# Low parts of feed-forward weight blocks: ScalarE and an adding transfer in VectorE's place, and 12 more blocks in seven products

## The chip, the cores and the metric

One core of one Trainium2 chip runs the whole program. The metric is the device time of one execution in microseconds; the time of a kernel is the median of its runs. The core has TensorE (PE: matmuls, and PEld, the weight loads beside them), VectorE (DVE), ScalarE (ACT), GpSimd (POOL) and SyncE (SP), which run side by side, each in the order of its own queue, and wait for one another by semaphores. Transfers are issued from a queue (before: SP's, and two from ACT's) and carried by 16 DMA engines.

## The reference

Two layers over x of 512 tokens by 1024 features, float32. Each has three sub-layers with a norm, a shift and scale made from a conditioning vector c, and a gated residual: a SwiGLU feed-forward, a mixer (convolutions in the first layer, pooling and block attention in the second), and a feed-forward again. Then a last norm. What the change touches is the feed-forward:

```python
def swiglu(h, w_gate, w_up, w_down):
    return (jax.nn.silu(h @ w_gate) * (h @ w_up)) @ w_down
...
mod = (cond @ ada_w[i] + ada_b[i]).reshape(bn, N_SUBLAYERS, 3, D_MODEL)
h = modulate(rms_norm(x, ffn_norm[i, 0]), mod[:, 0, 0], mod[:, 0, 1])
x = x + 0.5 * mod[:, 0, 2][:, None, :] * swiglu(h, ffn_w_gate[i, 0], ffn_w_up[i, 0], ffn_w_down[i, 0])
```

There are four feed-forwards, with 2816 inner columns (22 blocks of 128), in this order: layer 0 before and after the convolutions, layer 1 before and after the attention. The text calls them the first to the fourth.

## The kernel before

Activations lie transposed, features on partitions, 512 tokens along the row. A product in float32 is made of three matmuls in fp32r: each operand is split into a high part (rounded) and a low part (the rest), and high x high, high x low and low x high are summed in PSUM (`mac`, lines 299 to 301). `split` makes the parts of a weight block: ScalarE casts the raw block to `whi` (line 284), then VectorE subtracts to give `wlo` (line 286).

A feed-forward runs in three sections of 8, 6 and 8 blocks (`SECTIONS`): in each, gate and up products make the section's columns (`th`, `tl`), then eight down products (d0 to d7) add to the residual `x` (line 988). An *item* is one such product: 8 (or 6) k-steps of three matmuls over 512 tokens. Some blocks of a section are instead run as a *pair* (`pair_run`): gate and up of one block taken together as a two-by-two block product in seven products in place of eight (a11, s2, s3, a12, s1, a22, s4; `seventh`, line 784, matmuls over 256 tokens). That needs sums of weight blocks (lines 762, 766, 770), splits of them (741, 744, 749, 753), and steps on the results: `u2` (VectorE, line 840, the text's u, then two ScalarE copies to `yy`, 842 and 843, after which s1 may write its bank), `cc` (847), the multiply (859). It also needs four operand *forms* of the activations per feed-forward (`forms`, lines 723 to 735). `pair_items` says how many blocks of each section are pairs: (0, 2, 8), (2, 6, 8), (2, 4, 8) and (2, 6, 8) for the four feed-forwards, 56 in all. The rest of a section's gate and up blocks come first, as items.

The order of the work is written out in a plan, and `run` walks it. Before each plan step it splits the weights of items up to three ahead (`AHEAD`), as far as the four weight buffers (`W_BUFS`) allow: a product's buffers are those of the product four before. Raw weights come in a ring of four tiles of 1 MB (`RAW_BUFS`), filled by SP in the order of first use; a tile is reloaded when its last reader is done. The modulation vectors (c times `ada_w`) of later sub-layers are made in the background: `ada_steps` gives four accumulating steps (lines 482, 484), a `fold` (497, 498) and a small matmul per 1024 columns, and `beside` and `slack` put them on VectorE between items, by a credit per item (`free`, in microseconds of the author's estimate) less each step's cost. None is put in while pairs run (`hold`). `lead_in` starts a section's first pair, in the last four items before it.

`boundary` carries one sub-layer into the next: the last down products in halves, the statistics (`stats`, with POOL's power of -1/2, line 554), and the new h (`apply`).

Of the kernel before, what the change touches and what calls it, by code (L numbers as in the profile page):

```python
# [8 lines left out]
F32 = mybir.dt.float32  # L9
F32R = mybir.dt.float32r  # L10
AF = mybir.ActivationFunctionType
ALU = mybir.AluOpType
# [30 lines left out]
class Item:  # L43


    def __init__(self, raw, cut, shape, post=None, rhs=None, korder=None, store=None):
        self.raw, self.cut, self.shape = raw, cut, shape
        self.post, self.rhs = post, rhs
        self.korder, self.store = korder, store
        self.hi = self.lo = self.ps = None  # L50
        self.left = 0
        self.pool_low = self.late = self.hold = False


class Pair:
# [13 lines left out]
class Trunk:  # L69
# [200 lines left out]
    def split(self, it):  # L270
        nk, m = it.shape
        src = it.cut(it.raw.tile)
        if it.store is None:
            parts = [[p.tile([P, 1024], F32R, name=n, tag=n)[:, 0:nk * m].rearrange(
                "p (a b) -> p a b", a=nk) for p, n in ((self.wp, "whi"), (self.wp, "wlo"))]]
            step = nk
        else:
            parts = [[t.rearrange("p (a b) -> p a b", b=m) for t in pair] for pair in it.store]
            step = S // m
        it.hi, it.lo = [], []  # L280
        for i, (hi, lo) in enumerate(parts):
            w = src[:, i * step:(i + 1) * step, :]
            n = w.shape[1]
            self.nc.scalar.copy(hi[:, 0:n, :], w)  # L284
            eng = self.nc.gpsimd if it.pool_low else self.nc.vector
            low = lambda eng=eng, lo=lo, hi=hi, w=w, n=n: eng.tensor_tensor(  # L286
                lo[:, 0:n, :], w, hi[:, 0:n, :].bitcast(F32), op=ALU.subtract)
            if it.hold:
                self.held.append(low)
            else:  # L290
                low()
            it.hi += [hi[:, a, :] for a in range(n)]
            it.lo += [lo[:, a, :] for a in range(n)]
# [235 lines left out]
    def square(self, k, sl):  # L529

        nc = self.nc
        if k == 0:
            nc.scalar.activation(self.acc[:, sl], self.x[k][:, sl], AF.Square)
            return
        sq = self.np_.tile([P, S], F32, name="sq", tag="sq")
        nc.scalar.activation(sq[:, sl], self.x[k][:, sl], AF.Square)
        if self.ending and k == 7 and sl.start > 0:
            self.sq7 = sq
            return
        self.defer(lambda: nc.vector.tensor_tensor(  # L540
            self.acc[:, sl], self.acc[:, sl], sq[:, sl], op=ALU.add))

    def stats(self, half):
        nc = self.nc
        ps = self.bank()
        for j in range(2):
            c = 2 * half + j
            terms = [self.acc] if half == 0 or not self.ending else [self.acc, self.sq7]
            for t in terms:
                nc.tensor.matmul(ps[:, j:j + 1], lhsT=t[:, c * P:(c + 1) * P], rhs=self.ones[:, 0:1],  # L550
                                 start=t is terms[0], stop=t is terms[-1])
# [265 lines left out]
    def pair_run(self, pairs, down):  # L817
# [15 lines left out]
                self.plan.append(("use", slot))  # L833

        def keep1(p):
            p.p1 = self.fp.tile([P, 256], F32, name="p1c", tag="p1c", bufs=1)
            nc.scalar.copy(p.p1, p.ab[:, 0:256])

        def u2(p):
# [95 lines left out]
    def beside(self, items, todo, bg, free):  # L935
# [9 lines left out]
            self.slack(bg, free - cost)  # L945
        self.room = len(bg)

    def swiglu_pairs(self, secs, pairs, bg, skip, fn=None, due=0):


        self.form, self.credit, self.room = {}, 0.0, len(bg)
        end = len(bg) - due
        forms = [(lambda kk=kk: self.call(lambda: self.forms(kk)), 4.6) for kk in range(4)]
        lead = [list(zip(self.lead_in(ps[0]), (2.5, 1.4, 1.9, 1.2))) if ps else [] for ps in pairs]
        for n, ((gu, down), ps) in enumerate(zip(secs, pairs)):
            nf, last = SECTIONS[n], n == len(secs) - 1
            gu = gu[skip if n == 0 else 0:2 * (nf - len(ps))]
            todo = lead[n] if gu else []
            if n == 0 and ps:
                todo = forms + [(None, 0)] * (len(gu) - 8) + todo  # L960
            self.beside(gu, todo, bg, 3.7)
            if n == 0:
                assert len(bg) <= end
                self.plan.append(("sync",))
            if ps:
                self.plan.append(("hold", True))
                self.pair_run(ps, down)
                self.plan.append(("hold", False))
                self.slack(bg, 3.0)
            if fn is not None and last:  # L970
                self.call(lambda: self.table(fn))
            todo = []
            if not last and len(pairs[n + 1]) == SECTIONS[n + 1]:
                todo = lead[n + 1]
            if n == 0 and not ps:
                todo = forms + todo
            self.beside(down[2 if ps else 0:6 if last else 8], todo, bg,
                        2.9 if last else 3.5 if nf == 8 else 2.3)
        self.plan.append(("sync",))
        while bg:  # L980
            self.call(*bg.pop(0)[:2])
            self.call(self.flush)
# [163 lines left out]
    def group_norm(self, r):  # L1146
        nc = self.nc
        _, j, y, stage, x = r
        if stage == 0:
# [1 line left out]
            nc.tensor.matmul(ps, lhsT=self.blk, rhs=y, start=True, stop=True)  # L1151
            nc.vector.tensor_tensor(y, y, ps, op=ALU.subtract)
            self.free(ps)
            r[4] = sq = self.np_.tile([P, S], F32, name="sq", tag="sq")
            nc.scalar.activation(sq, y, AF.Square)
        elif stage == 1:
            ps = self.bank()
# [8 lines left out]
            r[4] = wide = self.np_.tile([P, S], F32, name="sq", tag="sq")  # L1166
# [115 lines left out]
    def pool_post(self, g):  # L1282
        nc = self.nc

        def go(ps, sl):
# [7 lines left out]
            w = 2 << g  # L1293

            def mean():
                o = self.np_.tile([P, S], F32, name="sq", tag="sq")
                nc.vector.scalar_tensor_tensor(o, cur[:, 16:], 1.0 / w, u[:, 16:],
                                               op0=ALU.mult, op1=ALU.subtract)
                nc.vector.tensor_tensor(o[:, 0:w], cur[:, 16:16 + w], self.rcnt[:, 0:w], op=ALU.mult)
                nc.vector.tensor_tensor(o[:, 0:w], o[:, 0:w], u[:, 16:16 + w], op=ALU.subtract)  # L1300
                self.defer(lambda: mix(o), 2)

            def mix(o):
                po = self.bank()
                nc.tensor.matmul(po, lhsT=self.pw[:, g, :], rhs=o, start=True, stop=True)
                b, sc = self.at["pool_b"] + g, self.at["pool_scale"] + g
                m = self.np_.tile([P, S], F32, name="sq", tag="sq")
# [163 lines left out]
    def start_spread(self):  # L1471
        nc = self.nc
        ps = self.bank()
        for c in range(4):
            nc.tensor.transpose(ps[:, c * P:(c + 1) * P],
                                self.rs[0][:, c:c + 1].to_broadcast([P, P]), self.ident)
        self.rb0 = self.np_.tile([P, S], F32, name="sq", tag="sq")
        nc.scalar.copy(self.rb0, ps)
        self.free(ps)

# [43 lines left out]
    def build(self):  # L1524
# [63 lines left out]

        bg = steps(0, (0, 2), (1, 1), (1, 0), (1, 2), (2, 1), (2, 0))
        bg.insert(6, (self.rest, None, 0.6))  # L1590
        self.swiglu_pairs(f[0, 0], self.pair_items(0, 0, (0, 2, 8)), bg, 7, AF.Sigmoid, 9)

        self.boundary_tail(f[0, 0], 1, z[:4])
        self.taps1, self.taps2, self.ready = [], [], []
# [26 lines left out]
        self.boundary(zo[6:], 2, g0[0][0][:4])  # L1621

        bg = steps(1, (0, 1), (0, 0), (0, 2))
        self.swiglu_pairs(g0, self.pair_items(0, 2, (2, 6, 8)), bg, 3)
        self.boundary(g0[-1][1][6:], 3, f[1, 0][0][0][:4], False)
        bg = steps(1, (1, 1), (1, 0), (1, 2), (2, 1))
        self.swiglu_pairs(f[1, 0], self.pair_items(1, 0, (2, 4, 8)), bg, 3, AF.Exp)

        self.boundary_tail(f[1, 0], 4, kq[:4])
        self.call(self.pm_consts)  # L1630
# [23 lines left out]
        self.mm(po[4])  # L1654
        self.mm(po[5])
        self.boundary(po[6:], 5, f[1, 2][0][0][:4])
        self.swiglu_pairs(f[1, 2], self.pair_items(1, 2, (2, 6, 8)), [], 3)
        tail = f[1, 2][-1][1][6:]
        self.call(lambda: setattr(self, "ending", True))
        self.call(lambda: self.scaled(range(5), FULL))  # L1660
# [99 lines left out]
```

## Time and profile before

| what | value |
|---|---|
| median of 3 runs | 1872.02 us (1871.92 to 1874.3) |
| the profiled execution | 1867.62 us, its span 1865.6 us |
| granted TensorE clock, mean | 0.989 of full speed |
| TensorE, VectorE, ScalarE, POOL busy | 97%, 77%, 43%, 7% |
| DMA | 247.52 MB, mean 133 GB/s, queue of SP 42.5% of 16 engines' span |

All times of the trace are in microseconds from the start of the span, those of single instructions partly in ns. The page gives busy shares of each engine, then the span in 40 slices of 46.6 us, then the chain of work that ended last, then groups of instructions by line. An engine's idle time in front of an instruction is put down to what released it.

### The profile page before, as it was taken

The numbers are of one execution on the slowest core, as the hardware profiler recorded it, in microseconds if no ns is written. First come the engines' busy times: TensorE is split into PE (matmuls) and PEld (weight loads), VectorE is DVE, ScalarE is ACT, GpSimd is POOL, SyncE is SP. The second block draws the span as 40 slices with busy tenths as digits, with TensorE's granted clock in tenths as the row PEclk, the third lists the DMA queues.
The fourth block names the chain that finished last, engine by engine and source line by source line (L and its number), as shares of the span: only waits on it lengthen the run. The fifth ranks groups of instructions, "written<-read, shape, count | busy, mean of one in ns | idle before, by whom it ended". The sixth has DMA issues, their size and how long they took to land.

```text
span 1865.6 us, 26636 instructions
## 1 busy us (share of the span) xinstructions
PE 1803.4 (97%) x10730; PEld 1566.0 (84%) x10730; DVE 1438.5 (77%) x2100; ACT 802.3 (43%) x1388; POOL 133.9 (7%) x107
## 2 busy tenths in 40 slices
PE   5999999999979999999999999999999999999998
PEld 4778889988758888989888889998876688898997
DVE  6689779788988868779678787886898577485874
ACT  4322335445544433535344234463545444253543
POOL 2100000005550000000000000000002000000000
PEclk7999999999989999999999999999999999999999
DMA  9585563433232346453423573543362132424321
GB/s 258 169 290 198 161 204 101 136 113 113 68 136 91 113 158 181 133 139 113 149 77 114 191 226 119 156 124 111 125 208 80 45 91 68 113 80 125 91 91 46
DMA packets 263234, 247.52 MB, mean 133 GB/s; under 512 B 5212, under 2 KB 243656, under 8 KB 263112
## 3 DMA queue, kind: packets, MB, share of 16 engines
q1 hardware_dynamic: 262980, 245.78, 42.5%
q8 instruction: 84, 1.38, 0.3%
q14 instruction: 38, 0.31, 0.0%
q10 hardware_dynamic: 132, 0.05, 0.0%
HBM read 243.72 MB, written 2.10 MB: 132 GB/s over the span
## 4 chain that ended last, share of the span: by engine, by line
PE 82%; DVE 12%; ACT 3%; issue 2%; POOL 1%; DMA 0%; SPq 0%; DVEq 0%; ACTq 0%; POOLq 0%
PE bank L784 27%; PE bank L299 17%; PE bank L301 17%; PE bank L300 17%; DVE hl L577 1%; DVE wlo L286 1%; DVE bank L1111 1%; PE bank L1378 1%; DVE wlo L753 1%; DVE t L572 1%; DVE adaacc L484 1%; ACT whi L284 1%; DVE s L762 1%; DVE acc L1501 1%; DVE yb L1043 0%
## 5 line engine op out<-in xcount | busy, mean ns | idle before, releaser
L299 PE MATMUL bank<-th,whi 128*128 128x512 f32 (+1 forms) x896 | 336.3, 375 | 5.2 <-ACT whi L284 4.5
L301 PE MATMUL bank<-th,wlo 128*128 128x512 f32 (+1 forms) x896 | 332.8, 371 | 5.4 <-POOL wlo L286 5.4
L300 PE MATMUL bank<-tl,whi 128*128 128x512 f32 (+1 forms) x896 | 332.8, 371 | 1.1 <-DVE tl L680 0.9
L299 PE MATMUL bank<-hh,whi 128*128 128x512 f32 (+1 forms) x864 | 322.3, 373 | 5.3 <-ACT hh L575 3.2
L300 PE MATMUL bank<-hl,whi 128*128 128x512 f32 (+1 forms) x864 | 316.8, 367 | 8.0 <-DVE hl L577 8.0
L301 PE MATMUL bank<-hh,wlo 128*128 128x512 f32 (+1 forms) x864 | 315.9, 366 | 2.5 <-DVE wlo L286 2.5
L284 ACT CAST whi<-raw 128x1024 fp32r<-128x1024 f32 (+1 forms) x205 | 203.9, 1010 | 136.3 <-PE bank L300 83.2
L286 DVE TENSOR_TENSOR wlo<-raw,whi 128x1024 fp32r<-128x1024 f32 (+1 forms) x195 | 235.0, 1220 | 26.5 <-ACT whi L284 25.7
L301 PEld LDWEIGHTS bank<-th,wlo 128*128 128x128 f32 x896 | 169.0, 189 | 38.5 <-POOL wlo L286 6.6
L299 PEld LDWEIGHTS bank<-th,whi 128*128 128x128 f32 x896 | 169.1, 189 | 38.0 <-ACT whi L284 5.6
L300 PEld LDWEIGHTS bank<-tl,whi 128*128 128x128 f32 x896 | 169.2, 189 | 32.2 <-DVE tl L680 1.3
L300 PEld LDWEIGHTS bank<-hl,whi 128*128 128x128 f32 x864 | 164.0, 190 | 37.9 <-DVE hl L577 9.5
L299 PEld LDWEIGHTS bank<-hh,whi 128*128 128x128 f32 x864 | 163.5, 189 | 37.5 <-ACT hh L575 3.3
L988 DVE SCALAR_TENSOR_TENSOR x<-bank,modG,x 128x512 f32<-128x512 f32 (+1 forms) x124 | 85.7, 698 | 141.1 <-PE bank L301 140.1
L301 PEld LDWEIGHTS bank<-hh,wlo 128*128 128x128 f32 x864 | 163.6, 189 | 32.2 <-DVE wlo L286 3.7
L784 PE MATMUL bank<-f,whi 128*128 128x256 f32 x896 | 163.7, 280 | 11.2 <-ACT yy L843 11.2
L784 PE MATMUL bank<-f,qhi 128*128 128x256 f32 x896 | 165.3, 282 | 0.0
L741 ACT CAST qhi<-raw 128x512 fp32r<-128x512 f32 x168 | 99.4, 618 | 118.4 <-issue 84.4
L784 PEld LDWEIGHTS bank<-f,whi 128*128 128x128 f32 x896 | 136.8, 188 | 13.4 <-ACT yy L843 13.4
L484 DVE SCALAR_TENSOR_TENSOR adaacc<-raw,cond,adaacc 128x1024 f32<-128x1024 f32 x112 | 143.7, 1283 | 2.7
L784 PEld LDWEIGHTS bank<-f,qhi 128*128 128x128 f32 x896 | 138.8, 190 | 0.0
L784 PE MATMUL bank<-f,qlo 128*128 128x256 f32 x448 | 126.4, 282 | 0.0
(245 smaller groups left out, 3317.8 us busy)
## 6 DMA issues: line engine op xcount, KB each, us to landing
raw<-in_ada_w_dram SPq DMA_DIRECT2D x64, 1024.0 KB, 5.3
raw<-in_ffn_w_down_dram SPq DMA_DIRECT2D x32, 1024.0 KB, 5.2
raw<-in_ffn_w_gate_dram SPq DMA_DIRECT2D x58, 512.0 KB, 4.0
raw<-in_ffn_w_up_dram SPq DMA_DIRECT2D x58, 512.0 KB, 5.3
raw<-in_ffn_w_gate_dram SPq DMA_DIRECT2D x15, 1024.0 KB, 5.4
raw<-in_ffn_w_up_dram SPq DMA_DIRECT2D x15, 1024.0 KB, 5.4
raw<-in_ffn_w_down_dram SPq DMA_DIRECT2D x16, 768.0 KB, 4.5
raw<-in_conv_w_in_dram SPq DMA_DIRECT2D x10, 1024.0 KB, 5.0
```

The costliest lines, as they stand in the source:

```text
L284: self.nc.scalar.copy(hi[:, 0:n, :], w)
L286: low = lambda eng=eng, lo=lo, hi=hi, w=w, n=n: eng.tensor_tensor(lo[:, 0:n, :], w, hi[:, 0:n, :].bitcast(F32), op=ALU.subtract)
L299: nc.tensor.matmul(ps, lhsT=it.hi[k], rhs=xh[:, sl], start=start, stop=False)
L300: nc.tensor.matmul(ps, lhsT=it.hi[k], rhs=xl[:, sl], start=False, stop=False)
L301: nc.tensor.matmul(ps, lhsT=it.lo[k], rhs=xh[:, sl], start=False, stop=stop)
L484: nc.vector.scalar_tensor_tensor(acc, r.tile[:, j, :], self.cond[:, k:k + 1], acc, op0=ALU.mult, op1=ALU.add)
L572: nc.vector.scalar_tensor_tensor(t, self.x[k][:, sl], self.modA[:, i, k:k + 1], rb, op0=ALU.mult, op1=ALU.mult)
L577: self.pend = lambda: nc.vector.scalar_tensor_tensor(self.hl[k][:, sl], t, b, self.hh[k][:, sl].bitcast(F32), op0=ALU.add, op1=ALU.subtract)
L741: self.nc.scalar.copy(hi, src)
L753: p.lows[names] = lambda: self.nc.vector.tensor_tensor(lo, src, hi.bitcast(F32), op=ALU.subtract)
L784: mm = lambda w, x, start=False: nc.tensor.matmul(ps, lhsT=w, rhs=x, start=start, stop=False, skip_group_check=True)
L988: nc.vector.scalar_tensor_tensor(self.x[d][:, sl], ps[:, sl], self.modG[:, i, d:d + 1], self.x[d][:, sl], op0=ALU.mult, op1=ALU.add)
```

## The change

For 116 items (`by_dma`: in each feed-forward the gate and up items of the first section from the fifth on, but in the first one from the ninth, and all down products) the low part is made otherwise: ScalarE writes -w, rounded, into `wlo`, and a transfer issued from POOL adds the raw block to it in place, SBUF to SBUF, which leaves w less its high part. The counts of pairs become (0, 6, 8), (4, 6, 8), (4, 6, 8) and (4, 6, 8), 68 in all. The credits per item rise by about one. `join` packs forms and lead-in where fewer items are left than they had. Some tiles move between pools, and the area for the descriptors of such transfers grows from 1024 to 4096 bytes a partition.

```diff
@@ split
-            if it.hold:
+            if it.by_dma:
+                self.nc.scalar.activation(lo[:, 0:n, :], w, AF.Copy, scale=-1.0)
+                self.nc.gpsimd.dma_start(lo[:, 0:n, :], w, accum_op=ALU.add)
+            elif it.hold:
                 self.held.append(low)
@@ square: a full-width square goes to a tile with tag "yy", a half to one of 256 columns
@@ pair_run
-            p.p1 = self.fp.tile([P, 256], F32, name="p1c", tag="p1c", bufs=1)
+            p.p1 = self.np_.tile([P, 256], F32, name="t256", tag="t", bufs=3)
@@ new
+    def join(self, forms, lead, n):
+
+        gap = n - len(forms) - len(lead)
+        if gap >= 0:
+            return forms + [(None, 0)] * gap + lead
+        out = [(None, 0)] * (n - 4) + lead
+        for e, (fn, cost) in enumerate(forms):
+            k = e * (n - 3) // len(forms)
+            f0, c0 = out[k]
+            if k < n - 4:
+                out[k] = (lambda a=f0, b=fn: (a and a(), b()), c0 + cost)
+            else:
+                last = forms[e:]
+                out[k] = (lambda b=f0: ([f() for f, _ in last], b()), c0 + cost * len(last))
+                break
+        return out
@@ swiglu_pairs
+        for it in secs[0][0][max(skip + 1, 4):] + sum((gu * (n > 0) + down for n, (gu, down) in enumerate(secs)), []):
+            it.by_dma = True
...
-                todo = forms + [(None, 0)] * (len(gu) - 8) + todo
-            self.beside(gu, todo, bg, 3.7)
+                todo = self.join(forms, todo, len(gu))
+            self.beside(gu, todo, bg, 4.7)
...
-                        2.9 if last else 3.5 if nf == 8 else 2.3)
+                        4.0 if last else 4.6 if nf == 8 else 3.2)
@@ build
-        self.swiglu_pairs(f[0, 0], self.pair_items(0, 0, (0, 2, 8)), bg, 7, AF.Sigmoid, 9)
+        self.swiglu_pairs(f[0, 0], self.pair_items(0, 0, (0, 6, 8)), bg, 7, AF.Sigmoid, 9)
...
-        self.swiglu_pairs(g0, self.pair_items(0, 2, (2, 6, 8)), bg, 3)
+        self.swiglu_pairs(g0, self.pair_items(0, 2, (4, 6, 8)), bg, 3)
...
-        self.swiglu_pairs(f[1, 0], self.pair_items(1, 0, (2, 4, 8)), bg, 3, AF.Exp)
+        self.swiglu_pairs(f[1, 0], self.pair_items(1, 0, (4, 6, 8)), bg, 3, AF.Exp)
...
-        self.swiglu_pairs(f[1, 2], self.pair_items(1, 2, (2, 6, 8)), [], 3)
+        self.swiglu_pairs(f[1, 2], self.pair_items(1, 2, (4, 6, 8)), [], 3)
...
-                    dynamic_dma_scratch_size=1024)
+                    dynamic_dma_scratch_size=4096)
```

The rows below are from the two kernels' instruction orders; the lines of each kernel are numbered by its own file.

ScalarE, start of the second feed-forward's first section, before and then in the changed kernel (`f` are the forms' casts, `sg` a gate product's silu, `th` an up product's high part; the `whi` and `wlo` rows are the weights of items to come, in the changed kernel the last of line 284 those of u3, and its line 756 casts the first pair's weights):

```order
L284 CAST whi<-raw 128x1024
L679 CAST th_118<-m 128x512
L734 CAST f_5396<-yy 128x512
L734 CAST f_5400<-yy 128x512
L284 CAST whi<-raw 128x1024
L672 ACTIVATE sg<-bank_5409 128x512
L734 CAST f_5447<-yy 128x512
L734 CAST f_5451<-yy 128x512
L284 CAST whi<-raw 128x1024
```

```order
L284 CAST whi<-raw 128x1024
L289 ACTIVATE wlo<-raw 128x1024
L686 CAST th_118<-m 128x512
L741 CAST f_5677<-yy 128x512
L741 CAST f_5681<-yy 128x512
L741 CAST f_5694<-yy 128x512
L741 CAST f_5698<-yy 128x512
L284 CAST whi<-raw 128x1024
L289 ACTIVATE wlo<-raw 128x1024
L679 ACTIVATE sg<-bank_5708 128x512
L741 CAST f_5747<-yy 128x512
```

Two casts of forms stood between an item's weights and the next; now four do, and line 289, the second pass, follows the casts of line 284.

VectorE, third feed-forward, from the end of the fourth down product of the first section towards the next section's first pair, before and then in the changed kernel (`x` rows end a down product each, `s` is the pair's first sum, `adaacc` and `adar` belong to the background modulation):

```order
L988 SCALAR_TENSOR_TENSOR x_96<-bank_9615,modG,x_96 128x512
L482 TENSOR_SCALAR adaacc<-raw,cond 128x1024
L484 SCALAR_TENSOR_TENSOR adaacc<-raw,cond,adaacc 128x1024 x3
L286 TENSOR_TENSOR wlo<-raw,whi 128x1024
L988 SCALAR_TENSOR_TENSOR x_97<-bank_9650,modG,x_97 128x512
L484 SCALAR_TENSOR_TENSOR adaacc<-raw,cond,adaacc 128x1024 x2
L519 SCALAR_TENSOR_TENSOR modA<-bank_9682,adabT 32x8 x4
L523 TENSOR_TENSOR modA<-modA,vec 128x8
L286 TENSOR_TENSOR wlo<-raw,whi 128x1024
L988 SCALAR_TENSOR_TENSOR x_98<-bank_9697,modG,x_98 128x512
```

```order
L1014 SCALAR_TENSOR_TENSOR x_96<-bank_10160,modG,x_96 128x512
L487 SCALAR_TENSOR_TENSOR adaacc<-raw,cond,adaacc 128x1024 x4
L1014 SCALAR_TENSOR_TENSOR x_97<-bank_10195,modG,x_97 128x512
L769 TENSOR_TENSOR s_10228<-raw 128x1024
L760 TENSOR_TENSOR wlo<-raw,whi 128x1024
L1014 SCALAR_TENSOR_TENSOR x_98<-bank_10234,modG,x_98 128x512
L773 TENSOR_TENSOR raw<-s_10228,raw 128x512
L777 SCALAR_TENSOR_TENSOR raw<-raw 128x512
L500 STREAM_TRANSPOSE yy<-adaacc 128x512
L501 TENSOR_REDUCE adar<-yy 128x16
```

The low parts of the down products (line 286) are gone from between these rows, and the next section's first pair has its first sum, low part and two sums there: before, that section began with four items and its first pair's sum came behind the row that ends d7 (`x_100`).

SP, the same place, before and then in the changed kernel (each gate and up row of 128 columns is half of a pair's raw tile, the other rows are one tile each):

```order
L268 DMA raw<-in_ffn_w_down_dram 128x8x256 x2
L268 DMA raw<-in_ada_w_dram 128x2x1024 x2
L268 DMA raw<-in_ffn_w_down_dram 128x8x256 x2
L268 DMA raw<-in_ada_w_dram 128x2x1024 x3
L268 DMA raw<-in_ffn_w_gate_dram 128x8x256
```

```order
L268 DMA raw<-in_ffn_w_down_dram 128x8x256 x3
L268 DMA raw<-in_ada_w_dram 128x2x1024 x2
L268 DMA raw<-in_ffn_w_down_dram 128x8x256
L268 DMA raw<-in_ada_w_dram 128x2x1024 x2
L261 DMA raw<-in_ffn_w_gate_dram 128x8x128
```

Two modulation tiles, not three, now stand between the last down tile (d6 and d7) and the next section's first gate tile.

## Rows read from the trace of the kernel before

**Rows 1.** The page, parts 1 and 2: busy times, then tenths in 40 slices

```profile
PE 1803.4 (97%) x10730; PEld 1566.0 (84%) x10730; DVE 1438.5 (77%) x2100; ACT 802.3 (43%) x1388; POOL 133.9 (7%) x107
...
PE   5999999999979999999999999999999999999998
...
DMA  9585563433232346453423573543362132424321
```

**Rows 2.** The page, part 4: chain that ended last, by engine, by line

```profile
PE 82%; DVE 12%; ACT 3%; issue 2%; POOL 1%; DMA 0%; SPq 0%; DVEq 0%; ACTq 0%; POOLq 0%
PE bank L784 27%; PE bank L299 17%; PE bank L301 17%; PE bank L300 17%; DVE hl L577 1%; DVE wlo L286 1%; DVE bank L1111 1%; PE bank L1378 1%; DVE wlo L753 1%; DVE t L572 1%; DVE adaacc L484 1%; ACT whi L284 1%; DVE s L762 1%; DVE acc L1501 1%; DVE yb L1043 0%
```

**Rows 3.** ScalarE by time, 690 to 730: start, duration, operation, idle before

```profile
697.56 1.06 ACT L284 CAST whi<-raw 128x1024 fp32r<-128x1024 f32 x1 [4.29 <-issue]
...
708.72 1.05 ACT L749 CAST whi<-raw 128x1024 fp32r<-128x1024 f32 x1 [4.49 <-PE bank L300]
```

**Rows 4.** VectorE by time, 726 to 758, inside a run of six pairs

```profile
737.47 0.69 DVE L847 TENSOR_TENSOR m<-bank,yy 128x512 f32<-128x512 f32 x1 [0.17 <-PE bank L784]
...
741.74 0.43 DVE L840 TENSOR_TENSOR bank<-bank,p1c 128x256 f32<-128x256 f32 x1 [0.71 <-PE bank L784]
...
757.11 0.69 DVE L847 TENSOR_TENSOR m<-bank,yy 128x512 f32<-128x512 f32 x1 [0.15 <-PE bank L784]
```

**Rows 5.** TensorE's waits (total, times, longest): span, 660-680, 1182-1260

```profile
PE bank L784 <- ACT yy L843: 11.2, 11, 2.8
...
PE bank L784 <- ACT yy L843: 0.9, 1, 0.9
...
PE bank L784 <- ACT yy L843: 0.3, 1, 0.3
```

**Rows 6.** TensorE by time, 730.9 to 734.5

```profile
731.24 0.28 PE L784 MATMUL bank<-hh,wlo 128*128 128x256 f32 x1
734.33 0.38 PE L784 MATMUL bank<-f,whi 128*128 128x256 f32 x1 [2.81 <-ACT yy L843]
```

**Rows 7.** VectorE by time, 726 to 734, start of that run

```profile
726.65 1.22 DVE L753 TENSOR_TENSOR wlo<-s,whi 128x1024 fp32r<-128x1024 f32 x1
727.78 2.60 DVE L484 SCALAR_TENSOR_TENSOR adaacc<-raw,cond,adaacc 128x1024 f32<-128x1024 f32 x2
...
733.16 0.43 DVE L840 TENSOR_TENSOR bank<-bank,p1c 128x256 f32<-128x256 f32 x1
```

**Rows 8.** The page, part 5: line, engine, operation, count, busy us, mean ns

```profile
L284 ACT CAST whi<-raw 128x1024 fp32r<-128x1024 f32 (+1 forms) x205 | 203.9, 1010 | 136.3 <-PE bank L300 83.2
L286 DVE TENSOR_TENSOR wlo<-raw,whi 128x1024 fp32r<-128x1024 f32 (+1 forms) x195 | 235.0, 1220 | 26.5 <-ACT whi L284 25.7
```

**Rows 9.** DMA issues: engine, count, KB each, median us to landing

```profile
raw<-in_ffn_w_gate_dram SPq DMA_DIRECT2D x58, 512.0 KB, 4.0
raw<-in_ffn_w_up_dram SPq DMA_DIRECT2D x58, 512.0 KB, 5.3
...
raw<-in_ada_w_dram SPq DMA_DIRECT2D x16, 512.0 KB, 8.0
```

**Rows 10.** Line 268, SP: duration ns min, median, max, first and last start

```profile
L268 SPq DMA_DIRECT2D raw<-in_ffn_w_down_dram x48: 367/368/368, 114.0 to 1802.6; - x48
```

**Rows 11.** VectorE by time, 614 to 640: one form, first step and behind

```profile
615.94 1.28 DVE L723 TENSOR_TENSOR s<-hh,hl 128x512 f32<-128x512 f32 x2
...
619.99 0.68 DVE L680 TENSOR_TENSOR tl<-m,th 128x512 fp32r<-128x512 f32 x1
```

**Rows 12.** VectorE by time, 690 to 727: a fold, from its first step

```profile
700.91 0.70 DVE L497 STREAM_TRANSPOSE yy<-adaacc 128x512 f32<-128x512 f32 x1
...
703.59 1.21 DVE L286 TENSOR_TENSOR wlo<-raw,whi 128x1024 fp32r<-128x1024 f32 x1
```

**Rows 13.** Windows: us, PE, PEld, DVE, ACT, POOL busy, clock, DMA share, GB/s

```profile
138.00:158.00 20.00, 19.12 (x83) 15.19 (x82) 17.11 (x24) 3.40 (x4) 0.00 (x0) 1.00 0.92 314
726.00:786.00 60.00, 57.19 (x489) 56.99 (x488) 52.51 (x69) 32.96 (x63) 0.00 (x0) 1.00 0.39 113
```

More of the change, by code (lines that the diff above doesn't have):

```diff
@@ L51, in __init__ @@
         self.left = 0
-        self.pool_low = self.late = self.hold = False
+        self.pool_low = self.late = self.hold = self.by_dma = False
 class Pair:
@@ L534, in square @@
             return
-        sq = self.np_.tile([P, S], F32, name="sq", tag="sq")
-        nc.scalar.activation(sq[:, sl], self.x[k][:, sl], AF.Square)
+        if sl == FULL:
+            sq = self.fp.tile([P, S], F32, name="yy", tag="yy", bufs=2)
+        else:
+            sq = self.np_.tile([P, 256], F32, name="sq", tag="sq")
+        nc.scalar.activation(sq, self.x[k][:, sl], AF.Square)
         if self.ending and k == 7 and sl.start > 0:
@@ L540, in square @@
         self.defer(lambda: nc.vector.tensor_tensor(
-            self.acc[:, sl], self.acc[:, sl], sq[:, sl], op=ALU.add))
+            self.acc[:, sl], self.acc[:, sl], sq, op=ALU.add))
     def stats(self, half):
@@ L549, in stats @@
             for t in terms:
-                nc.tensor.matmul(ps[:, j:j + 1], lhsT=t[:, c * P:(c + 1) * P], rhs=self.ones[:, 0:1],
+                e = j if t is not self.acc else c
+                nc.tensor.matmul(ps[:, j:j + 1], lhsT=t[:, e * P:(e + 1) * P], rhs=self.ones[:, 0:1],
                                  start=t is terms[0], stop=t is terms[-1])
@@ L946, in beside @@
         self.room = len(bg)
+    def join(self, forms, lead, n):
[8 more added lines that the diff above has]
+                out[k] = (lambda a=f0, b=fn: (a and a(), b()), c0 + cost)
+            else:
+                last = forms[e:]
+                out[k] = (lambda b=f0: ([f() for f, _ in last], b()), c0 + cost * len(last))
+                break
+        return out
     def swiglu_pairs(self, secs, pairs, bg, skip, fn=None, due=0):
@@ L1153, in group_norm @@
             self.free(ps)
-            r[4] = sq = self.np_.tile([P, S], F32, name="sq", tag="sq")
+            r[4] = sq = self.fp.tile([P, S], F32, name="sqw", tag="sqw", bufs=2)
             nc.scalar.activation(sq, y, AF.Square)
@@ L1165, in group_norm @@
             nc.gpsimd.tensor_tensor(rs, ms, self.mhalf, op=ALU.pow)
-            r[4] = wide = self.np_.tile([P, S], F32, name="sq", tag="sq")
+            r[4] = wide = self.fp.tile([P, S], F32, name="sqw", tag="sqw", bufs=2)
             nc.scalar.copy(wide.rearrange("p (a b) -> p a b", a=8), rs[:, :, None].to_broadcast([P, 8, 64]))
@@ L1295, in mean @@
             def mean():
-                o = self.np_.tile([P, S], F32, name="sq", tag="sq")
+                o = self.fp.tile([P, S], F32, name="sqw", tag="sqw", bufs=2)
                 nc.vector.scalar_tensor_tensor(o, cur[:, 16:], 1.0 / w, u[:, 16:],
@@ L1306, in mix @@
                 b, sc = self.at["pool_b"] + g, self.at["pool_scale"] + g
-                m = self.np_.tile([P, S], F32, name="sq", tag="sq")
+                m = self.fp.tile([P, S], F32, name="sqw", tag="sqw", bufs=2)
                 nc.vector.tensor_scalar(m, po, self.vec[:, b:b + 1], self.vec[:, sc:sc + 1],
@@ L1476, in start_spread @@
                                 self.rs[0][:, c:c + 1].to_broadcast([P, P]), self.ident)
-        self.rb0 = self.np_.tile([P, S], F32, name="sq", tag="sq")
+        self.rb0 = self.fp.tile([P, S], F32, name="yy", tag="yy", bufs=2)
         nc.scalar.copy(self.rb0, ps)
```

## The prediction

> **What bounds the kernel now.** I read the page from the top, then the chain of waits, then stretches of the timeline. TensorE is busy 97% of the span and its digits are 9 in nearly every slice, VectorE 77%, ScalarE 43%, POOL 7% [rows 1]. Busy matmuls could still wait for one another, so the chain decides: 82% of it is TensorE, the seven-product line alone 27%, VectorE 12% [rows 2]. The reader is to see that matmul columns are the bill, and that a helper engine matters only where a product starts late. Two prices of a block of 128 feed-forward columns follow. As two ordinary products: ScalarE's casts of the next weights at 697.56 and 708.72, two products apart, each released by TensorE, give 5.58 a product, **11.16 us a block** [rows 3]. In seven products: the same VectorE step of pairs two apart starts at 737.47 and 757.11, so **9.82 us a block** [rows 4].
>
> Late starts are the other thing to see. In the list of waits TensorE's seven-product line waited for ScalarE's copy `yy` 11 times, 11.2 us together, 2.8 at most [rows 5]; there are 11 pair runs, so it is once per run, in front of the first pair's product s1. The longest begins after the matmul at 731.24 [rows 6]. Its cause stands in VectorE's timeline: between the low part at 726.65 and the step u (L840) at 733.16 lie two accumulations of the modulation, 2.60 us, and u releases `yy` [rows 7]. A matmul's own pace there is 0.11 us, and the gap between the two starts is 3.09, so the wait is 3.0, 0.2 above its row; with the same 0.2 on the others [rows 5] the waits that I need are **3.0 us** (twice, both in the second feed-forward), **1.1** and **0.5**.
>
> **The change part by part.**
>
> *12 blocks move to seven products* (56 to 68 pairs; the order has 432 more matmul rows, which is 12 x (84 - 48)). 12 x (11.16 - 9.82) = **-16.1 us**, all on the path, if the pairs' helpers keep pace: VectorE still idles 0.71 and 0.17 us within a pair [rows 4].
>
> *116 low parts leave VectorE* for ScalarE and a POOL transfer. VectorE is spared 116 x 1.22 us [rows 8], off the path except where VectorE is late. ScalarE gains 116 x about 1.0 us [rows 8] at 43% busy; between two casts it idles 4.3 to 4.5 us at a time [rows 3], which covers this; without that cover each pass would be 1.0 us. What the change adds is a wait: TensorE's third matmul of a product now waits for a transfer that no row shows.
>
> *The transfer's latency L* (issue to landing of 512 KB, adding in place). Nearest rows: loads of the same size from DRAM land after 4.0 us alone, 5.3 us behind their partner, and 8.0 us where they queue [rows 9]. An issue on SP takes 0.37 us [rows 10]. I take 5.3 + 0.4 = 5.7 us, since each transfer shares the engines with weight loads; the ends are 4.4 and 8.4 us. The Trainium skill, "DMA: Bandwidth & Descriptors" (Anatomy of one DMA — SWDGE (gpsimd) path), gives such a POOL transfer about 2.0 us plus its bytes at 436 GB/s, an estimate of 3.2 us for 512 KB; by that the sum below would be near -14 us. No row here shows one.
>
> *Lead.* Four weight buffers and splits three products ahead give a product's low part the time of three products, 16.7 us for eight-row blocks, less 2 x 1.0 for the two ScalarE passes [rows 3, 8]. L of 5.7 hides there, and 8.4 too. Two places have less.
>
> First, **the start of the first section** in the second, third and fourth feed-forward. Four pairs leave fewer ordinary products, and `join` packs the four operand forms two by two. Say zero is the end of product u1. A form takes VectorE 4.05 us [rows 11], so two end at 8.7; only then can ScalarE, which has their casts in its queue, make the weights of u3: 8.3 + 2.0 + L = 16.0, and u3 wants its low part at 17.2. Hidden, by 1 us. VectorE goes on: tail 0.6, two forms to 17.4, s and wlo 2.3, multiply 0.6, two sums 1.4, tail and q 1.2, multiply 0.6 (u3 ends at 22.3), wlo, tail, q, s, wlo, u 5.0, ScalarE 0.75: about 29.2, against 22.3 + 4 x 1.4 = 27.9 for s1. A wait of 1.3 instead of 1.1, three times: **+0.6**.
>
> Second, **the join from the first section's down products to the next pairs** in the second and third feed-forward. The first pair's weights need the raw tile that the last down block leaves (order: SP). Say zero is the end of down product d1. d3 ends at 11.2 and frees the buffers for d7: two passes 2.0, then L, then the load 5.3: the pair's first sum runs at 18.5 + L. From there to `yy` VectorE's order holds s and wlo 2.3, x 0.67, two sums 1.3, a fold 2.7, x and q 1.3, four accumulations 4.6, x 0.67, wlo 1.1, the modulation 0.9, q 0.6, s, wlo and u 2.6, ScalarE 0.75: 19.5 (low parts by [rows 8], accumulations by [rows 7], the fold by [rows 12]; the small ones are estimates by width from these). So s1 may start at 38 + L = 43.7, and TensorE is there at 33.6 + 5.6 = 39.2: a wait of 4.5 where the second had 3.0 and the third 1.1: **+1.5 and +3.4**.
>
> Other joins, by the same count from the end of the last down product: second feed-forward, last section: x, wlo, q, s, wlo, u, yy 5.8 against 5.6, so 0.5 where 3.0 stood, **-2.5**. First feed-forward, last section: a fold now stands in that chain, 8.5 against 5.6, so 2.9 for 0.5, **+2.4**; its run of two pairs is now one of six, 1.1 to 0.5, **-0.6**. The third feed-forward's tail takes over a modulation chunk that ran earlier: after d4 VectorE holds x, 5.2 of accumulations, sums, a fold 2.7 and two low parts, about 15.3 us, against 13.3 when the statistics' matmul wants its input: **+2**.
>
> *Moved at no cost:* buffer renamings (cover: the tags already rotate; without it some 0.3 us of ScalarE), POOL's rs steps, now behind the transfers (cover: the last transfer is issued three products before; without it one issue, 0.4 us), and the 4096-byte descriptor area.
>
> Sum: -16.1 + 0.6 + 1.5 + 3.4 - 2.5 + 2.4 - 0.6 + 2 = **-9.3 us**. The profiled execution took 1867.6 (span 1865.6), so 1858.3; the median of the three runs, 1872.0, lies 4.4 above it, so **1862.7**. At L = 4.4 two joins give back 2.6 (-11.9). At L = 8.4 they cost 5.4 more and u3 waits 1.5 us three times: +0.6. The point of no gain is L of about 8.2.
>
> **The rivals.**
>
> *A. The transfer is slow because each byte is read twice, source and destination.* Then 2 x 5.3 + 0.4 = 11 us. Joins +10.6, u3 waits 4.1 us three times, +12.3, and d2 behind six-row pairs, whose lead is 10.3 us, waits 2.3 us four times, +9.2: -9.3 + 32.1 = **+22.8, 1894.8**. It decides from L of about 8.2. For it: the 16 DMA engines' share is already 0.92 at 138 to 158 in the first feed-forward [rows 13], where the first of the transfers fall. Against: the share is 0.39 at 726 to 786 [rows 13], and three products of lead cover most of them. The Trainium skill, "Collectives: The Full Stack" (The bandwidth ceiling: the fold count and why AG ≠ RS ≠ AR), says an adding transfer needs two source reads and so runs at half a copy's rate; by that rule it is this rival, and no row of this kernel shows an adding transfer.
>
> *B. POOL's issue is the bound.* Source rows are pieces of 512 B, 1024 of them. If POOL takes over 5.6 us for one, it falls behind TensorE; in a run of six with some 9 us of slack it decides from about 7 us. At 8 us: 6 x 2.4 - 9 = 5 us in each of 12 stretches is 60, the sixteen in a row of the first feed-forward give 28, and some 8 of the waits of [rows 5] go: **+80, about 1950**. Against: POOL is 7% busy [rows 1]; nothing shows its price.
>
> *C. The transfers land after 8 us in the crowd, and the gains are eaten:* -1 to +2, **1872**.
>
> *D. L is 4.4, and VectorE, relieved, also covers the fold and the tail (2.4 + 2.0):* -11.9 - 4.4 = **-16.3, 1855.7**.
>
> That the blocks do not change is excluded by the order.
>
> **How the numbers follow.** Forecast (L 4.4 to 7) 0.48; D 0.12; C 0.12; A 0.18; B 0.10. For the forecast: the loads' own rows and the idle engines; for A and B, that the one new wait has no row. The time is 1862.7, that of the likeliest. The range leaves out B and the upper part of A, and below it what lies beyond D: 1855 to 1888. Its own range is 1860 to 1869. Faster by over 0.2% (3.7 us, about what a measurement tells from no change): forecast and D, 0.60. Within: C, 0.12. Slower: A and B, 0.28.
>
> **What would show it.** Right: seven-product blocks still 9.82 us apart, 11 runs of pairs with one wait each, TensorE's idle before an ordinary product's third matmul near zero, POOL's transfers landing in 4.4 to 7 us, VectorE's low parts down by 116. Wrong: TensorE waiting for the DMA queue of POOL at many products (A), POOL's instructions back to back (B), or the seven-product pace growing because VectorE idles nowhere in the pairs.

## The result, and the profile after

The changed kernel takes **2122.35 us** (median of 4 runs, 2116.03 to 2123.21) against 1872.42 before: ratio 1.1325, 95% interval 1.1302 to 1.1349, 250 us slower. I had forecast 1862.7, 1855 to 1888.

The page of the changed kernel, parts 1 and 2 (columns as in [rows 1]):

```profile
PE 1867.0 (88%) x11162; PEld 1620.0 (76%) x11162; DVE 1377.6 (65%) x2080; ACT 934.3 (44%) x1588; POOL 311.8 (15%) x223
...
PE   6966998978989897989978979898699998999997
...
PEclk7988999999999998999999989999899999999999
DMA  9689777484224658494665594947654125757455
```

TensorE fell from 97% to 88%, VectorE is relieved as announced (1438.5 to 1377.6 us although 12 blocks of seven-product work came to it), ScalarE has its second pass. The DMA row is up nearly everywhere, and TensorE's clock row has lost 9s in the feed-forwards. TensorE's list of waits, with the four largest (engine, line, what it waited for: total, times, longest), answers to [rows 5]:

```profile
PE bank L304 <- DMA wlo<-raw: 154.7, 56, 8.4
PE bank L506 <- DVE adar L501: 16.7, 2, 11.1
PE bank L791 <- ACT yy L850: 11.1, 10, 2.5
PE bank L303 <- DVE hl L584: 8.0, 6, 1.6
```

The first line is the largest part of the loss: the third matmul of 56 products (line 304) waited for the transfer, 154.7 us. The waits before s1 (`yy`), on which most of my working went, are 11.1 us as before. TensorE's timeline in one stretch of eight down products, the second feed-forward's first (start, duration, operation, idle before):

```profile
798.31 0.50 PE L304 MATMUL bank<-th,wlo 128*128 128x512 f32 x1 [1.67 <-DMA wlo<-raw]
805.04 0.50 PE L304 MATMUL bank<-th,wlo 128*128 128x512 f32 x1 [0.87 <-DMA wlo<-raw]
814.76 0.80 PE L304 MATMUL bank<-th,wlo 128*128 128x512 f32 x1 [3.86 <-DMA wlo<-raw]
834.86 0.80 PE L304 MATMUL bank<-th,wlo 128*128 128x512 f32 x1 [6.29 <-DMA wlo<-raw]
```

The lateness grows along the stretch: 1.67 and 0.87, then 3.86 and 6.29. That is a queue, not one late transfer. The transfers' line (instructions with duration ns min/median/max, POOL's idle time by what ended it, and the time from issue to landing):

```profile
L290 POOL DMA_DIRECT2D wlo<-raw x116: 1436/1558/1748, 84.8 to 2092.6; - x116
...
  issue: 225.1, 37
...
DMA to landing us min/median/max: 5.5/6.7/14.3
```

The median latency of a transfer was near what I took, 6.7 for 5.7 us, though 31 of the 116 landed later than my upper end of 8.4. But 37 times POOL sat idle, 6.1 us each, for nothing that the profile names. POOL's timeline in that same stretch (384 KB and 768 pieces each in the second fence, which is from the first feed-forward's second section):

```profile
776.61 1.56 POOL L290 DMA_DIRECT2D wlo<-raw  x1 [44.21 <-ACT t L844]
783.61 1.57 POOL L290 DMA_DIRECT2D wlo<-raw  x1 [5.44 <-PE bank L791]
790.35 1.56 POOL L290 DMA_DIRECT2D wlo<-raw  x1 [5.17 <-issue]
798.58 1.57 POOL L290 DMA_DIRECT2D wlo<-raw  x1 [6.68 <-ACT whi L284]
```

```profile
286.65 1.45 POOL L290 DMA_DIRECT2D wlo<-raw  x1 [60.93 <-ACT t L844]
288.49 1.44 POOL L290 DMA_DIRECT2D wlo<-raw  x1 [0.39 <-PE bank L791]
293.84 2.93 POOL L290 DMA_DIRECT2D wlo<-raw  x2 [3.91 <-ACT wlo L289]
```

These large transfers start 6.7 to 8.2 us apart (in the other stretches up to 14.6), an issue of 1.56 us and then a pause; two small ones start 1.8 us apart or back to back. The landings tell what the pause is for: the transfers begun at 776.61, 783.61 and 790.35 land after 6.7, 6.4 and 7.9 us, and the next begins 0.3 us behind each landing. Of the 84 large ones none begins while another transfer is under way. Products end 5.58 us apart [rows 3]. So eight large transfers fall behind eight products.

The clock is the other part. The mean granted clock fell from 0.989 to 0.948 of 2.4 GHz (the rest is stretches at 1.2 GHz; in the timeline above the matmuls behind the waits of 3.86 and 6.29 us took 0.80 us, those behind the short ones 0.50). In clock time lost that is (1 - 0.948) x 2119.8 = 110 us against (1 - 0.989) x 1865.6 = 21 us, 90 us more, some of it under waits. What is not under waits shows beside the version without the transfer (e2 below), which has the same 11162 matmuls: TensorE is busy 1867.0 us here and 1793.3 there, 74 us more, and idle 252.8 us for 70.4, 182 us more. Together that is the 256 us between their spans.

### The profile page after: what moved, and what is told of

Same layout as the page of the kernel before. It is cut to its first block, busy times and chain, and to the rows that moved or that the text cites. A ratio compares the mean times of both kernels' runs of the same rounds, so it can differ in the third digit from the quotient of the medians.

```text
span 2119.8 us, 28089 instructions
## 1 busy us (share of the span) xinstructions
PE 1867.0 (88%) x11162; PEld 1620.0 (76%) x11162; DVE 1377.6 (65%) x2080; ACT 934.3 (44%) x1588; POOL 311.8 (15%) x223
## 3 DMA queue, kind: packets, MB, share of 16 engines
q1 hardware_dynamic: 275460, 245.78, 38.4%
q0 software_dynamic: 112448, 56.63, 23.3%
## 5 line engine op out<-in xcount | busy, mean ns | idle before, releaser
L290 POOL DMA_DIRECT2D wlo<-raw x116 | 177.9, 1533 | 1393.3 <-ACT t L844 752.6
L304 PE MATMUL bank<-hh,wlo 128*128 128x512 f32 (+1 forms) x672 | 246.6, 367 | 39.5 <-DMA wlo<-raw 36.8
L302 PE MATMUL bank<-hh,whi 128*128 128x512 f32 (+1 forms) x672 | 251.5, 374 | 5.5 <-ACT hh L582 3.2
L303 PE MATMUL bank<-hl,whi 128*128 128x512 f32 (+1 forms) x672 | 245.0, 365 | 8.0 <-DVE hl L584 8.0
L791 PE MATMUL bank<-f,whi 128*128 128x256 f32 x1088 | 200.9, 282 | 11.1 <-ACT yy L850 11.1
L791 PE MATMUL bank<-f,qhi 128*128 128x256 f32 x1088 | 203.6, 285 | 3.8 <-ACT qhi L748 3.8
L304 PEld LDWEIGHTS bank<-hh,wlo 128*128 128x128 f32 x672 | 130.3, 194 | 67.6 <-DMA wlo<-raw 43.8
L791 PEld LDWEIGHTS bank<-f,qhi 128*128 128x128 f32 x1088 | 171.0, 193 | 4.0 <-ACT qhi L748 4.0
L791 PE MATMUL bank<-f,wlo 128*128 128x256 f32 x544 | 154.7, 284 | 5.6 <-DVE wlo L760 5.5
L303 PEld LDWEIGHTS bank<-hl,whi 128*128 128x128 f32 x672 | 130.8, 195 | 30.3 <-DVE hl L584 9.5
## 6 DMA issues: line engine op xcount, KB each, us to landing
raw<-in_ffn_w_down_dram SPq DMA_DIRECT2D x16, 768.0 KB, 11.2
```

The lines of the kernel that those rows point to most:

```text
L290: self.nc.gpsimd.dma_start(lo[:, 0:n, :], w, accum_op=ALU.add)
L302: nc.tensor.matmul(ps, lhsT=it.hi[k], rhs=xh[:, sl], start=start, stop=False)
L303: nc.tensor.matmul(ps, lhsT=it.hi[k], rhs=xl[:, sl], start=False, stop=False)
L304: nc.tensor.matmul(ps, lhsT=it.lo[k], rhs=xh[:, sl], start=False, stop=stop)
L791: mm = lambda w, x, start=False: nc.tensor.matmul(ps, lhsT=w, rhs=x, start=start, stop=False, skip_group_check=True)
```

## The experiments

"Before" was run beside each group, medians 1868.6 to 1870.6 us, and each ratio is to the "before" of its own group. Where the time lies is read from one table: the length of each feed-forward in the profile, from the second of POOL's two rs steps at one boundary (line 554 before) to the first at the next, the first one from the span's start.

| kernel | runs, us | ratio (interval) | first | second | third | fourth | clock |
|---|---|---|---|---|---|---|---|
| before | 1870.5 | 1 | 401.3 | 350.0 | 348.8 | 344.5 | 0.989 |
| changed | 2122.4 | 1.1325 (1.1302, 1.1349) | 495.4 | 406.1 | 416.1 | 377.9 | 0.948 |
| e1 room for two | 2013.3 | 1.0761 (1.0734, 1.0788) | 453.8 | 386.3 | 396.4 | 349.8 | 0.958 |
| e2 no transfer | 1865.2 | 0.9976 (0.9962, 0.9989) | 401.0 | 343.5 | 351.7 | 341.9 | 0.985 |
| e3 VectorE | 1881.8 | 1.0065 (1.0042, 1.0089) | 410.1 | 346.5 | 357.5 | 342.9 | 0.985 |
| e4 old counts | 2189.8 | 1.1709 (1.1684, 1.1735) | 518.9 | 420.0 | 436.1 | 392.0 | 0.935 |
| e5 contiguous | 1931.0 | 1.0328 (1.0310, 1.0346) | 433.1 | 359.8 | 371.8 | 343.4 | 0.973 |
| e6 halves | 1941.3 | 1.0379 (1.0354, 1.0403) | 434.9 | 359.9 | 372.4 | 344.1 | 0.977 |
| e7 every other | 1894.1 | 1.0132 (1.0112, 1.0152) | 417.4 | 350.8 | 361.0 | 342.9 | 0.983 |
| e8 4 blocks | 1874.5 | 1.0031 (1.0019, 1.0043) | 400.0 | 356.7 | 348.8 | 342.9 | 0.988 |
| e9 no modulation loads | 1897.8 | 1.0147 (1.0132, 1.0163) | 410.2 | 353.2 | 359.0 | 348.4 | 0.983 |
| e10 4 blocks, credits | 1867.0 | 0.9988 (0.9978, 0.9998) | 401.4 | 350.3 | 348.7 | 342.9 | 0.989 |
| e11 POOL | 1902.1 | 1.0174 (1.0158, 1.0189) | 423.1 | 350.3 | 361.5 | 346.9 | 0.978 |
| e12 last item free | 1861.6 | 0.9955 (0.9942, 0.9969) | 401.4 | 346.1 | 348.8 | 343.2 | 0.989 |

**Is it the transfers, and which property of them?** (e1 to e4)

```diff
 e1: -  dynamic_dma_scratch_size=4096    +  dynamic_dma_scratch_size=4288
 e2: -  self.nc.gpsimd.dma_start(lo[:, 0:n, :], w, accum_op=ALU.add)
 e3: -  it.by_dma = True                 +  it.by_dma = False
 e4: -  (0, 6, 8) (4, 6, 8) (4, 6, 8) (4, 6, 8)   +  (0, 2, 8) (2, 6, 8) (2, 4, 8) (2, 6, 8)
```

> One edit to the changed kernel: the descriptor area grows from 4096 to 4288 bytes a partition. Theory R (room): in the changed kernel POOL issues the next transfer of 1024 pieces only after the one before has landed (6.72 us apart at best, 13 to 14 beside weight loads, against 5.58 a product), while two of 768 pieces are issued 1.5 us apart; so the area holds one large transfer and two small ones. With a little more room two large ones are under way at once: issues come 1.5 to 2 us apart, TensorE's 155 us of waits for the low part fall below 40, time 1860 to 1920. Theory E (engines): a transfer keeps all 16 DMA engines busy for 4.1 to 4.9 us, eight of them 37 us in a stretch of eight down products, 45 us long, with four weight tiles of 1 MB and the modulation's beside them; then two under way only share the engines, each lands later, and the time stays above 2050.

> The adding transfer is left out: the low part stays the negated, rounded weight, so the third matmul multiplies other numbers of the same shape. R and E alike: all of the loss goes, and what is left is the change without its wait; by the prediction's sum with a latency of zero (the two joins no longer wait) about -17 us, 1850 to 1862. Theory V (order and joins: the packed forms, the second ScalarE pass, the ring of raw tiles are late whatever the transfer does): above 1950.

> All 116 low parts go back to VectorE; 68 pairs, the packed joins and the higher credits stay. R and E: no wait for a transfer is left; VectorE gets 116 x 1.22 = 141 us back in the same order and is late in places, 1860 to 1900. V: above 1950.

> The counts of pairs go back to the 56 of before, the 116 transfers stay. R and E: the loss is the transfers', so it stays and the 12 blocks' 16 us are missing: 2120 to 2150. V: the loss came with the counts and the packed joins, below 1950.

Without the transfer, or with VectorE in its place, the loss is gone (1865.2, 1881.8): order, joins and ScalarE's second pass are not it. With the old counts it grew to +319 us, for here 140 items go by transfer, not 116 as I wrote: 2.3 us each, near 250/116 = 2.2 in the changed kernel; that is above the forecast of both theories (2120 to 2150), which had the count wrong. So V falls.

192 bytes a partition more took 109 us off. POOL's timeline in e1, at the stretch shown above, and TensorE's first wait:

```profile
733.11 1.56 POOL L290 DMA_DIRECT2D wlo<-raw  x1 [49.84 <-ACT t L844]
735.26 1.56 POOL L290 DMA_DIRECT2D wlo<-raw  x1 [0.60 <-DVE bank L847]
```

```profile
PE bank L304 <- DMA wlo<-raw: 63.8, 20, 5.8
```

The second issue follows after 2.15 us in place of 7.0, and 67 of the 84 large transfers now begin with one other under way, none with two: R is right that the area held one large transfer at a time. But 63.8 us of waits are left and the time is 143 us over before, where R said below 40 us and at most 1920, so R alone is too small; E said above 2050, so E alone is too large. The fourth feed-forward is nearly whole again (+5.3 us), the first three are not (+52, +36, +48). What those have and the fourth has not is the background modulation with its loads.

**The engines** (e9, e5, e6, e7)

```diff
 e9 (on e1): -  acc, r.tile[:, j, :], self.cond[:, k:k + 1], acc   +  acc, acc, self.cond[:, k:k + 1], acc   (and no load of r)
 e5: -  dma_start(lo, w, accum_op=ALU.add)   +  dma_start(lo, hi, accum_op=ALU.add)
 e6: -  raw tile (k, 256), one load          +  raw tile (2, k, 128), two loads
 e7: -  all down and first-section items     +  down[1::2] of each section
```

> The kernel with room for two (4288 bytes), without the 1 MB loads of the background modulation: VectorE's accumulating steps stay, at the same places and of the same size, but read what is already there, so the modulation's values are not the reference's. C (what is left of the loss with room for two is the 16 DMA engines shared with these loads): the first three feed-forwards fall to the fourth's +5 each, the first a little more, 1885 to 1920. Otherwise (the transfer itself, or VectorE's steps, are late): the time stays above 1980.

> The transfer adds the high part (which lies in one piece of 4 KB a partition) in place of the raw block (eight pieces of 512 B): same bytes, 128 pieces for 1024; the low parts come out as about zero, which is not the reference's sum. P (a transfer is paid by the piece, in the area as on the engines): it lands in 3 to 4.5 us, issues follow ScalarE, 5.6 us apart, no wait of TensorE for it: 1860 to 1890. B (it is paid by the byte, read twice): landing stays near 6 us or more, one at a time, above 2050.

> The raw tiles of items with a transfer are loaded as two halves, so that each block lies in one piece of 4 KB a partition; the arithmetic is the reference's. The price is that these loads come in pieces of 512 B in place of 1 KB. P: TensorE's waits for the low part go, the loads take longer (512 B pieces, two issues), 1865 to 1900. B: above 2050.

> Transfers for every second down product only (48 for 116), the others on VectorE; area of 4096 bytes as in the changed kernel. R: one transfer per 11.2 us is under POOL's 6.7, so no queue forms; only those beside weight loads (13 us) come near the lead of 16.7: 1870 to 1900. E: each transfer costs in proportion, 48/116 of 250 us, about 1975.

e9 came out inside its forecast: without the modulation's loads, VectorE's steps kept, the loss with room for two falls from 143 to 27 us (+8.9, +3.2, +10.2, +3.9 by feed-forward). So the second cause is that transfers and the modulation's loads run together. That they meet in the 16 engines is read from the engines' bill; e9 by itself does not show it, since these loads also leave the ring of four raw tiles, where SP waits for transfers to land before it reloads. Those waits of SP are no shorter in e9 (523.5 us for 513.2 in e1), which speaks against the ring, but no run separates the two. The bill stands on the page, part 3 (queue, kind: packets, MB, share of 16 engines), of the changed kernel and then of e5:

```profile
q1 hardware_dynamic: 275460, 245.78, 38.4%
q0 software_dynamic: 112448, 56.63, 23.3%
```

```profile
q0 software_dynamic: 16704, 56.63, 15.8%
```

By its packets' time a transfer holds all 16 engines for 0.233 x 2119.8 / 116 = 4.26 us (56.63 MB / 116 = 0.488 MB on average; 4.6 for one of 512 KB), one of contiguous pieces for 0.158 x 1930.6 / 116 = 2.63 us. Loads take 0.384 x 2119.8 / 245.78 = 3.31 us per MB, 1.62 us for the same bytes. A stretch of eight down products, 44.7 us, asks for 8 x 4.6 + 4 x 3.5 (its four tiles) = 51 us before the modulation has any. The engines are full there, as windows of e1 show (as in [rows 13]) around the first such stretch of the second feed-forward, with modulation, and of the fourth, without:

```profile
733.00:790.00 57.00, 50.93 (x242) 41.63 (x241) 20.23 (x23) 17.95 (x23) 12.48 (x8) 0.94 1.05 207
1727.00:1772.00 45.00, 45.00 (x231) 37.64 (x230) 12.50 (x17) 19.59 (x26) 12.48 (x8) 1.00 1.15 187
```

The share is packets' time and can pass 1. In the fourth TensorE never idles all the same; in the second the modulation's bytes come on top, and it idles 6 us. With e5's transfers it is 8 x 2.8 + 14 = 36 us, which fits without the modulation (fourth feed-forward 343.4) and not beside it. The landings in e5, from the page's DMA issues (engine, count, KB, median us), show who pays:

```profile
raw<-in_ada_w_dram SPq DMA_DIRECT2D x64, 1024.0 KB, 10.6
wlo<-whi POOLq DMA_DIRECT2D x84, 512.0 KB, 8.5
```

The modulation's tiles land after 10.6 us (5.1 in the changed kernel, whose transfers are held back by the queue): P's times for e5 and e6 were too low, since I had counted waits for the transfer only; its landing of 3 to 4.5 us was too low as well. e6, whose sums are those of the changed kernel, comes to 10 us more than e5. In e7 one transfer per 11.2 us made no queue that TensorE felt: it waited for a transfer but once, 2.8 us. It costs 25.5/48 = 0.5 us a transfer instead of 2.2, as R said and E did not, and e3, with the same order and no transfer, has 11 of the 25. It does not choose between room and engines, for at this rate the engines have time to spare too.

**Versions without a transfer** (e11, e8, e10, e12)

```diff
 e11: -  it.by_dma = True   +  it.pool_low = True
 e8:  -  by_dma; 68 pairs; credits up   +  none; (0, 2, 8) (4, 6, 8) (2, 4, 8) (4, 6, 8); credits of before
 e10: e8, in the second and fourth feed-forward 4.7 per gate/up item and +1.1 per down item
 e12: e10 with +1.6 per down item, and there in beside
+        if not (self.spare_last and todo and n == len(items) - 1):
             self.slack(bg, free - cost)
```

> No transfers: POOL itself subtracts for the 116 items (2.37 us each where it does so in the kernel before, against 5.58 us a product), 68 pairs, joins and credits of the change. If POOL keeps pace and disturbs nobody: the result of the run without transfers, 1860 to 1868. If POOL and VectorE slow each other (one of VectorE's low parts took 2.3 us for 1.2): VectorE late in joins, 1875 to 1910.

> No transfers, low parts on VectorE, credits and counts of before, except (4, 6, 8) in the second and fourth feed-forward: four more blocks in seven products. At 1.34 us a block -5.4 us; the packed start and joins there and the third run above say -3.4 and -1.6: 1864 to 1868. If VectorE is late with the forms packed two by two, no gain.

> As the run with four more blocks and no transfers, but in the second feed-forward 1.1 us more credit per item, so that no modulation step is left for its end (there TensorE waited 11.6 us for a fold, and the second feed-forward took 356.7 us). If that wait ate the gain: second feed-forward about 344, fourth 343, total 1860 to 1865. If VectorE is late elsewhere instead: no gain, 1868 or more.

> As the run with four more blocks and higher credits (second feed-forward 350.3 us, waits of 3.7 and 1.4 us before the first pair's product s1), but in the second and fourth feed-forward no modulation step follows the last item before a pair run, where two accumulations, 2.6 us, held up the step u; 0.5 us more credit on the others makes room. If those accumulations are what is late, the waits before s1 in the second feed-forward fall to 0.5 to 1 us each, its time to about 346, the whole to 1862 to 1865. If a fold or a low part takes their place, no change from 1867.

In e11 POOL subtracts in time and is hardly waited for (5.9 us, before 5.4), but VectorE slows beside it. VectorE's accumulating steps in e11, then in e2, where POOL has no low parts (count | busy us, mean ns):

```profile
L487 DVE SCALAR_TENSOR_TENSOR adaacc<-raw,cond,adaacc 128x1024 f32<-128x1024 f32 x112 | 177.5, 1585 | 4.7 <-DMA raw<-in_ada_w_dram 1.8
```

```profile
L486 DVE SCALAR_TENSOR_TENSOR adaacc<-raw,cond,adaacc 128x1024 f32<-128x1024 f32 x112 | 143.7, 1283 | 4.3 <-DMA raw<-in_ada_w_dram 1.5
```

That is 112 x 0.30 = 34 us of VectorE's time. The kernel loses 32, but that the two are the same microseconds is not shown: most of these steps are off the path, and TensorE's waits for the folds behind them are 16.5 us for e2's 5.7. e8 gained its 1.6 in the fourth feed-forward and lost 6.7 in the second, to a fold left for the end; its forecast (1864 to 1868) missed. A wait of TensorE in the second feed-forward, 590 to 960, in e8, in e10 and in e12, each time the one with the longest single wait:

```profile
PE bank L506 <- DVE adar L501: 11.4, 1, 11.4
```

```profile
PE bank L791 <- ACT yy L850: 6.4, 3, 3.6
```

```profile
PE bank L791 <- ACT yy L850: 2.9, 3, 1.6
```

The credits of e10 took the fold away, but the waits for `yy` there rose from 2.2 us in e8 to 6.4 (before: 6.5), so the second feed-forward came to 350.3 where I had said 344, and the whole missed its forecast of 1860 to 1865. Leaving the last item free then took the accumulations from in front of u [rows 7], and the waits fell to 2.9. **e12, 1861.6 us, ratio 0.9955 (0.9942 to 0.9969), beats both kernels**, with four more blocks and no transfer.

## Why the prediction was wrong, point by point

**What bounds, and the blocks: right.** One reading slipped without harm: of the two casts that gave 5.58 us a product, the first is put down to `issue`, not to TensorE [rows 3]. The seven-product pace held, by the rows that answer to [rows 4] (9.82 a block):

```profile
754.11 0.69 DVE L854 TENSOR_TENSOR m<-bank,yy 128x512 f32<-128x512 f32 x1 [0.19 <-PE bank L791]
...
763.93 0.69 DVE L854 TENSOR_TENSOR m<-bank,yy 128x512 f32<-128x512 f32 x1 [0.16 <-PE bank L791]
```

**The latency: right in the median, too narrow in its range.** 5.7 us taken, ends 4.4 and 8.4; median 6.7, beside loads up to 14.3, and 31 of 116 above 8.4. The Trainium skill, "DMA: Bandwidth & Descriptors" (Anatomy of one DMA — SWDGE (gpsimd) path), led to an estimate of 3.2 us. The trace does not agree: no transfer of 512 KB landed in under 6.4 us, and none of 384 KB in under 5.5.

**The lead: this is the step that failed.** I wrote that a transfer has "the time of three products, 16.7 us", and "L of 5.7 hides there, and 8.4 too". That treats each as if it were alone. Eight follow one another, and what decides then is the interval of one transfer against that of one product: 6.7 to 14 us against 5.58. Three products of lead only delay the first wait. I had no row for the interval and put none into the sum; the 4096-byte descriptor area, on which it hangs, stands there under "moved at no cost", the only one of the three without a cover. The runs show two causes of the interval, taken off in this order: the room for one large transfer (109 us by e1) and the modulation's loads beside the transfers (116 us more by e9, 2013.3 to 1897.8), by the bill above in the engines; 33 us are left between e9 and e2, by inference the transfers beside weight loads.

**The rivals.** B had the right shape (one at a time, behind from 5.6 us on) for a wrong reason: POOL's own issue is 1.56 us, it is the room that holds it. Its price of 80 us was too low by the factor of the intervals beside loads and by the clock, its chance of 0.10 too. A's cost is real, but on the engines and not as a latency: 4.26 and 2.63 us of engine time against 1.62 for a load; that a second read makes it is not shown. The Trainium skill, "Collectives: The Full Stack" (The bandwidth ceiling: the fold count and why AG ≠ RS ≠ AR), says of ReduceScatter that its add needs two source reads and so has half the rate of a plain gather. By e5's 2.63 to 1.62 the trace agrees roughly for contiguous pieces; for pieces of 512 B it is worse, 2.6 times. The measure is a rough one, since the loads come in pieces of 0.9 KB on average (245.78 MB in 275460 packets) and from DRAM. I read it as 11 us of latency, where it is a share of the engines. The DMA shares that I quoted [rows 13] were the place to add it up: 116 x 4.3 us.

**The clock: no term at all.** TensorE's waits came back as stretches at 1.2 GHz, 90 us of clock time; 74 us of longer busy time against e2 are its share outside the waits. Small waits do it too, in e2: TensorE's waits, then windows (as in [rows 13]) around them.

```profile
284.36 0.79 PE L790 MATMUL bank<-f,whi 128*128 128x256 f32 x2 [3.76 <-ACT yy L849]
...
1293.64 0.60 PE L505 MATMUL bank<-adar,sel 128*128 128x32 f32 x2 [5.70 <-DVE adar L500]
```

```profile
270.00:290.00 20.00, 16.24 (x106) 15.01 (x105) 18.38 (x26) 7.78 (x13) 0.00 (x0) 0.91 0.57 154
...
1280.00:1305.00 25.00, 19.30 (x116) 17.39 (x114) 16.58 (x30) 4.09 (x6) 0.68 (x1) 0.86 0.50 169
```

In the kernel before both windows stand at 1.00.

**The other terms**, tested by e2, where the latency is zero (1865.2 us, forecast 1850 to 1862). My sum is then -17.3 us: -3.6, -7.5, -3.8 and -2.5 by feed-forward. Measured: -0.3, -6.5, +2.9 and -2.6, and the first mixer, which the change does not touch, 4.5 longer (0.70 of full clock at 535 to 560, against 0.86 before). The second and the fourth, where the joins' working lies, are right within 1 us. The first had its wait behind the fold (3.8, I said 2.9), the third its fold at the end (5.7, I said 2), and both the clock behind them.

What stays open: what stretches single transfers to 14.3 us beside loads, how much room other sizes need, how much of e9's 116 us is the engines and how much the ring of raw tiles, and whether the 33 us between e9 and e2 are all weight loads; none of it was tried.

## What to carry to other kernels

Price a new transfer three times: its latency, the interval at which its queue can start the next, and the time it holds the DMA engines, added to what they carry already in that stretch. A lead of some products hides a latency, never an interval longer than a product. And to a wait of several microseconds on TensorE add the clock that falls behind it; the cheap gain was in the order, in the last item before a run.

## What was not expected of the hardware

192 bytes of descriptor area were worth 109 us: with 4096 bytes never more than one adding transfer of 1024 pieces was under way, with 4288 two. By packets' time an adding transfer in pieces of 512 B cost the engines 2.6 times what the loads here took for the same bytes, in pieces of 3 to 4 KB 1.6 times. With POOL subtracting beside it an accumulating step of VectorE took 1585 ns on average for 1283.
